# Choosing the experts of the last block's second and third tile beside the dense experts

## The chip, the cores and the metric

The kernel runs on one core of a Trainium2 chip. The metric is the device time of one execution in microseconds (us), lower is better.

## The reference

One decoder layer is computed for 1024 prompt tokens and 64 sample tokens, model width 1024, all in float32. A recurrent branch and a windowed attention branch are merged into a residual stream `hres`. Then comes the part that this change touches, an expert layer in which every token takes 8 heads times 16 experts out of 128 x 128, each expert being one row of `expert_u` and one of `expert_v`:

```python
s = einsum('nhpd,hpkd->nhpk', qr, sub_keys)           # two scores lists of 128 per head
s_top, i_top = top_k(s, 16)
cand = s_top[:, :, 0, :, None] + s_top[:, :, 1, None, :]
best, pos = top_k(cand, 16)                            # 16 of the pairs
idx = take_along_axis(i_top[0] * 128 + i_top[1], pos)  # 128 experts of a token
g = softmax(best)
act = gelu(einsum('cd,ced->ce', xt, expert_u[idx])) * g
y = hres + einsum('ce,ced->cd', act, expert_v[idx])
```

## The kernel before

**Blocks and tiles.** The tokens are worked through in three blocks (`BLOCKS`, line 42): 256 prompt tokens with the 64 sample tokens, then 384 and 384 prompt tokens. A tile is 128 tokens on the 128 partitions; the last block has three tiles. For each block the trunk (line 296) ends with `retrieve` (line 753), which leaves the two top-16 lists of each head and token in `v16` and `i16`.

**The choice.** `choose` (line 778) makes `idx` and `g` from these lists, one tile after the other. For a tile, DVE adds the pairs into `cd` and their indices into `ce` (line 799, 14 instructions), takes the best 16 for each of 8 heads with max, index and replace (lines 809 to 814, 64 instructions), and recovers the indices with a subtraction `eq` and a reduction `ev` for each head (lines 823, 825). A softmax follows (lines 834 to 839), with one exponential on ACT. For the last block the results go into the tiles `gA` and `iA` (lines 839, 841), which stay on the chip. `choose` is a generator with a `yield` after each head of either loop, 16 a tile. Its scratch tiles have one buffer each, so a tile's pieces wait for those of the tile ahead. In the first two blocks `behind` (line 992) lets it run next to the following block's trunk, there beside gathers for the sample tokens (`early_u`, line 962, and `early_v`, line 977).

**Two kinds of expert work.** The 640 prompt tokens of the first two blocks are done densely in `dense` (line 1014): all 128 groups of 128 experts are loaded, split into a high and a low part (`split`, line 160: high on ACT, low on POOL as `ul` and `vl`), and multiplied with all tokens on PE, three groups of experts in turn (`GRP`). DVE multiplies the scores with the routing weights (line 1052), makes the low part `al` (line 164), and adds the products into `dac` (lines 1070, 1072). The loads `un`, `vn` and `gt` are issued by SP.

The 384 tokens of the last block are done by gathering (`gather_steps`, line 876). For each tile there are 128 steps that fetch one row of `expert_u` for every token (an indirect DMA issued by POOL, line 888, four buffers `row`) and take its product with the token on DVE (line 890), and then 128 steps that fetch a row of `expert_v` (line 900) and add it into `acc` (line 902). A tile begins with a load of its tokens into `st` (line 881), which ACT copies to `xt` (line 883); it ends with ACT copying `acc` to `st` and SP storing it to `y` (line 906). `st` has two buffers.

**The order.** The code names `choose` for the whole last block first, in a pool of its own (`xp2`, line 1020), which is closed before the pool `gp` of the gathers is opened (line 1024), so that both lie in the same memory. Then comes the loop over the dense experts, and after each expert's `vl` a number of gather steps are named (`pump`, line 1062), 768 steps over 120 experts, with the rule that POOL takes them behind that `vl` (line 1061). The order on each engine's queue is set when the program is built: a scheduler plays a timeline and gives an engine, of the instructions that are ready, the one named first. On the chip each engine works through its own queue in that order.

Of the kernel before, what the change touches and what calls it, by code (L numbers as in the profile page):

```python
# [8 lines left out]
F32 = mybir.dt.float32  # L9
# [10 lines left out]
P = 128  # L20
D = 1024
# [11 lines left out]
NSLOT = PH * TOPK  # L33
# [8 lines left out]
BLOCKS = [(0, 256, True), (256, 640, False), (640, 1024, False)]  # L42
# [32 lines left out]
class Kern:  # L75
# [702 lines left out]
    def choose(self, bi):  # L778
# [6 lines left out]
        for t, (c0, r) in sorted(enumerate(tiles), key=lambda x: x[1][1]):  # L785
# [53 lines left out]
            nc.vector.tensor_tensor(gv[0:r], bv[0:r], sz[0:r].unsqueeze(2).to_broadcast([r, PH, TOPK]), op=ALU.mult)  # L839
            if r0 == RA:  # L840
                nc.vector.tensor_copy(self.iA[:, t], ev)
                continue
            e32 = xp.tile([P, NSLOT], I32, tag="bi", name="e32", bufs=1)
            nc.vector.tensor_copy(e32[0:r], ev[0:r].rearrange("p h s -> p (h s)"))
# [31 lines left out]
    def gather_steps(self, gp, gps):  # L876
        nc, i, o = self.nc, self.i, self.o
        for t in range(NA // P):

            st = gp.tile([P, D], F32, tag="st", name="st", bufs=2)  # L880
            nc.sync.dma_start(st, self.xn2n_d[t * P:(t + 1) * P, :])
            xt = gps.tile([P, D], F32, tag="gx", name="xt", bufs=1)
            nc.scalar.copy(xt, st)
            hv = gp.tile([P, NSLOT], F32, tag="hv", name="hv", bufs=2)
            ia = self.iA[:, t].rearrange("p h s -> p (h s)")
            for s in range(NSLOT):
                row = gp.tile([P, D], F32, tag="row", name="row", bufs=4)
                nc.gpsimd.indirect_dma_start(out=row, out_offset=None, in_=i["expert_u"],  # L888
                                             in_offset=bass.IndirectOffsetOnAxis(ap=ia[:, s:s + 1], axis=0))
                nc.vector.scalar_tensor_tensor(row, row, 1.0, xt, op0=ALU.mult, op1=ALU.mult, accum_out=hv[:, s:s + 1])  # L890
                yield
            nc.scalar.activation(hv, hv, AF.Gelu_apprx_tanh)
            nc.vector.tensor_tensor(hv, hv, self.gA[:, t].rearrange("p h s -> p (h s)"), op=ALU.mult)
            st = gp.tile([P, D], F32, tag="st", name="st", bufs=2)
            nc.sync.dma_start(st, self.hres_d[RA + t * P:RA + (t + 1) * P, :])
            acc = gps.tile([P, D], F32, tag="gx", name="acc", bufs=1)
            nc.scalar.copy(acc, st)
            for s in range(NSLOT):
                row = gp.tile([P, D], F32, tag="row", name="row", bufs=4)
                nc.gpsimd.indirect_dma_start(out=row, out_offset=None, in_=i["expert_v"],  # L900
                                             in_offset=bass.IndirectOffsetOnAxis(ap=ia[:, s:s + 1], axis=0))
                nc.vector.scalar_tensor_tensor(acc, row, hv[:, s:s + 1], acc, op0=ALU.mult, op1=ALU.add)  # L902
                yield
            st = gp.tile([P, D], F32, tag="st", name="st", bufs=2)
            nc.scalar.copy(st, acc)
            nc.sync.dma_start(o["y"][RA + t * P:RA + (t + 1) * P, :], st)

# [106 lines left out]
    def dense(self):  # L1014
        tc, nc, i, o = self.tc, self.nc, self.i, self.o
        halves = [(0, COL0[1]), (COL0[1], ND)]
        with ExitStack() as cx:
            up = cx.enter_context(tc.tile_pool(name="up", bufs=2))
            vp = cx.enter_context(tc.tile_pool(name="vp", bufs=GRP + 1))
            with tc.tile_pool(name="xp2", bufs=1) as self.xp:  # L1020
                for _ in self.choose(len(BLOCKS) - 1):
                    pass
            gps = cx.enter_context(tc.tile_pool(name="gps", bufs=1, space=PSUM))
            self.steps = self.gather_steps(cx.enter_context(tc.tile_pool(name="gp", bufs=1)), gps)
            ngat = 2 * NSLOT * (NA // P)
            done = 0
            psc = cx.enter_context(tc.tile_pool(name="dpsc", bufs=3, space=PSUM))
            pou = cx.enter_context(tc.tile_pool(name="dpou", bufs=3, space=PSUM))
            ac = [self.bp.tile([P, 4, ND], F32, tag="bl", name="dac0"), up.tile([P, 4, ND], F32, tag="dac", name="dac1", bufs=1)]
            groups = [list(range(s, min(s + GRP, P))) for s in range(0, P, GRP)]  # L1030
            for gi, grp in enumerate(groups):
                acts = []
                for e in grp:
                    uh = up.tile([P, KD, P], F32R, tag="uh", name="uh")
                    ul = up.tile([P, KD, P], F32R, tag="ul", name="ul")
                    un = up.tile([P, KD, P], F32, tag="raw", name="un", bufs=3)
                    nc.sync.dma_start(un, i["expert_uT"][e])
                    self.split(uh, ul, un, nc.gpsimd)
                    if e % 4 == 0:
                        gts = []  # L1040
                        for a, b in halves:
                            gts.append(up.tile([P, 12, 4, CH], F32, tag="gt", name="gt", bufs=3)[:, 0:(b - a) // CH])
                            nc.sync.dma_start(gts[-1], self.g_d[a // CH:b // CH, :, e:e + 4, :].rearrange("c j e n -> j c e n"))
                    ah = vp.tile([P, ND], F32R, tag="ah", name="ah")
                    al = vp.tile([P, ND], F32R, tag="al", name="al")
                    for (a, b), gt in zip(halves, gts):
                        ps = psc.tile([P, 512], F32, tag="sc", name="sc")
                        self.mm3(ps[:, 0:b - a], [(uh[:, k, :], ul[:, k, :], self.dx[k // 4][:, k % 4, a:b], self.dx[2 + k // 4][:, k % 4, a:b]) for k in range(KD)])
                        ge = ps[:, 0:b - a]
                        nc.scalar.activation(ge, ge, AF.Gelu_apprx_tanh)  # L1050
                        gv = ge.rearrange("j (c n) -> j c n", n=CH)
                        nc.vector.tensor_tensor(gv, gv, gt[:, :, e % 4, :], op=ALU.mult)
                        self.split(ah[:, a:b], al[:, a:b], ge)
                    vh = vp.tile([P, D], F32R, tag="vh", name="vh")
                    vl = vp.tile([P, D], F32R, tag="vl", name="vl")
                    vn = up.tile([P, D], F32, tag="raw", name="vn", bufs=3)
                    nc.sync.dma_start(vn, i["expert_v"][e * P:(e + 1) * P, :])
                    vsub = self.split(vh, vl, vn, nc.gpsimd)
                    acts.append((vh, vl, ah, al))
                    want = min(ngat, -(-ngat * (e + 1) // PACE))  # L1060
                    with tc.issue_after(vsub.ins):
                        self.pump(want - done)
                    done = max(done, want)
                for k in range(KD):
                    c = slice(k * P, (k + 1) * P)
                    for a, b in halves:
                        ps = pou.tile([P, 512], F32, tag="ou", name="ou")
                        self.mm3(ps[:, 0:b - a], [(vh[:, c], vl[:, c], ah[:, a:b], al[:, a:b]) for vh, vl, ah, al in acts])
                        if gi == 0:
                            nc.vector.tensor_copy(ac[k // 4][:, k % 4, a:b], ps[:, 0:b - a])  # L1070
                        else:
                            nc.vector.tensor_tensor(ac[k // 4][:, k % 4, a:b], ac[k // 4][:, k % 4, a:b], ps[:, 0:b - a], op=ALU.add)  # L1072
            for _ in self.steps:
                pass

            for t0 in range(0, ND, P):
                r = P
                y0 = t0 if t0 < COL0[1] else t0 - COL0[1] + ROW0[1]
                yt = up.tile([P, D], F32, tag="raw", name="yt", bufs=3)
                nc.sync.dma_start(yt[0:r], self.hres_d[y0:y0 + r, :])  # L1080
                for h in range(2):
                    pt = psc.tile([P, 4, P], F32, tag="sc", name="tr")
                    for k in range(4):
                        nc.tensor.transpose(pt[0:r, k, :], ac[h][:, k, t0:t0 + r], self.ident)
                    ys = yt[0:r, h * 512:(h + 1) * 512]
                    nc.vector.tensor_tensor(ys, ys, pt[0:r].rearrange("p k d -> p (k d)"), op=ALU.add)
                nc.sync.dma_start(o["y"][y0:y0 + r, :], yt[0:r])
# [116 lines left out]
```

## Time and profile before

| | us |
|---|---|
| median of 3 runs | 3814.39 |
| lowest of them | 3812.35 |
| the profiled execution, its own time | 3815.67 |
| its span, first to last instruction | 3813.9 |

| engine | busy over the span |
|---|---|
| PE (TensorE, products) | 3395.1 us, 89% |
| DVE (VectorE) | 2890.5 us, 76% |
| POOL (GpSimd) | 1535.9 us, 40% |
| ACT (ScalarE) | 1454.7 us, 38% |

The execution took 3815.67 us, 1.77 us more than its span. The trunk lasts to about 1820 us of the span; the dense experts and the gathers fill the rest. Times in rows are us from the span's start unless marked ns. In a row of a timeline stand start, duration, engine, line, operation, tile written and tiles read, and in brackets how long the engine had been idle and what ended that. In a row of stretches, the numbers behind those of the engines are the granted clock of PE, the mean busy share of the DMA engines and the GB/s they moved.

### The profile page before, as it was taken

To read this page: it belongs to the slowest core of one execution; us is meant where nothing else is said; L and a number is where in the kernel's file an instruction comes from. 1 tells how busy PE (TensorE), PEld (TensorE's weight loads), DVE (VectorE), ACT (ScalarE), POOL (GpSimd) and SP (SyncE) were. 2 spreads that over 40 slices of the span, in tenths; PEclk is the share of its full clock that TensorE was granted. 3 is DMA by queue.
4 is the path that set the end of the run, shared out by engine and by line. 5 is a ranking of instruction groups with operands and counts; after the bars stand their busy time and mean duration, and the time that the engine had idled before them with its cause. 6 is when DMAs were issued, how large, how long until landed. Compare 5 with 4: busy or idle time off the path is not lost.

```text
span 3813.9 us, 59344 instructions
## 1 busy us (share of the span) xinstructions
PE 3395.1 (89%) x21891; PEld 3238.4 (85%) x21891; DVE 2890.5 (76%) x6727; ACT 1454.7 (38%) x2969; POOL 1535.9 (40%) x1240
## 2 busy tenths in 40 slices
PE   6899989778898988678899999999999999999990
PEld 6789978668895878677799999999999999999990
DVE  6566897998789974557977776777777777777786
ACT  4565454446755372774322222222222222222210
POOL 0011100440000222000357776777767776777764
PEclk8899999889998999888899999999999999999995
DMA  6388823776561999654358988899888998998988
GB/s 227 121 258 283 263 77 106 251 233 199 187 210 44 305 311 343 212 189 143 123 203 312 324 304 290 305 318 324 304 299 305 314 322 316 315 323 311 309 293 282
DMA packets 539235, 968.36 MB, mean 254 GB/s; under 512 B 38108, under 2 KB 356508, under 8 KB 535840
## 3 DMA queue, kind: packets, MB, share of 16 engines
q0 software_dynamic: 141120, 513.86, 37.6%
q1 hardware_dynamic: 397824, 450.70, 36.9%
q8 instruction: 172, 2.82, 0.3%
q14 instruction: 119, 0.97, 0.1%
HBM read 860.10 MB, written 105.99 MB: 253 GB/s over the span
## 4 chain that ended last, share of the span: by engine, by line
PE 39%; DMA 20%; DVE 17%; issue 11%; POOL 7%; ACT 6%; SPq 0%; POOLq 0%; DVEq 0%; ACTq 0%
DMA row<-in_expert_v,iA 7%; PE mm L183 6%; PE mm L185 6%; PE mm L184 6%; DMA row<-in_expert_u,iA 4%; PE ou L183 3%; PE ou L184 3%; PE ou L185 3%; PE sc L183 2%; PE sc L184 2%; PE sc L185 2%; POOL row L888 2%; DVE acc L902 2%; PE tr L922 2%; ACT oij L942 2%
## 5 line engine op out<-in xcount | busy, mean ns | idle before, releaser
L183 PE MATMUL ou<-ah,vh 128*128 128x256 f32 (+1 forms) x2048 | 633.3, 314 | 47.2 <-ACT ah L163 27.8
L183 PE MATMUL sc<-dx,uh 128*128 128x256 f32 (+1 forms) x2048 | 636.1, 311 | 13.7 <-ACT uh L163 8.7
L184 PE MATMUL ou<-al,vh 128*128 128x256 f32 (+1 forms) x2048 | 632.5, 311 | 3.1 <-DVE al L164 2.9
L185 PE MATMUL sc<-dx,ul 128*128 128x256 f32 (+1 forms) x2048 | 634.3, 310 | 1.0 <-POOL ul L164 1.0
L184 PE MATMUL sc<-dx,uh 128*128 128x256 f32 (+1 forms) x2048 | 634.9, 310 | 0.0
L185 PE MATMUL ou<-ah,vl 128*128 128x256 f32 (+1 forms) x2048 | 630.7, 310 | 0.0
L902 DVE SCALAR_TENSOR_TENSOR acc<-row,hv,acc 128x1024 f32<-128x1024 f32 x384 | 493.9, 1286 | 146.7 <-DMA row<-in_expert_v,iA 138.4
L890 DVE SCALAR_TENSOR_TENSOR row<-row,xt 128x1024 f32<-128x1024 f32 x384 | 465.5, 1217 | 149.0 <-DMA row<-in_expert_u,iA 134.7
L900 POOL DMA_INDIRECT row<-in_expert_v,iA x384 | 360.7, 939 | 278.8 <-DVE acc L902 199.6
L164 POOL TENSOR_TENSOR ul<-un,uh 128x1024 fp32r<-128x1024 f32 x128 | 308.6, 2411 | 384.1 <-DMA gt<-g_d 303.6
L888 POOL DMA_INDIRECT row<-in_expert_u,iA x384 | 360.8, 940 | 247.7 <-DVE row L890 176.5
L183 PEld LDWEIGHTS ou<-ah,vh 128*128 128x128 f32 x2048 | 385.7, 190 | 63.1 <-ACT ah L163 33.8
L183 PEld LDWEIGHTS sc<-dx,uh 128*128 128x128 f32 x2048 | 391.6, 191 | 15.4 <-ACT uh L163 9.0
L184 PEld LDWEIGHTS ou<-al,vh 128*128 128x128 f32 x2048 | 389.7, 191 | 5.4 <-DVE al L164 4.8
L185 PEld LDWEIGHTS sc<-dx,ul 128*128 128x128 f32 x2048 | 390.8, 191 | 1.5 <-POOL ul L164 1.5
L184 PEld LDWEIGHTS sc<-dx,uh 128*128 128x128 f32 x2048 | 391.3, 191 | 0.0
L185 PEld LDWEIGHTS ou<-ah,vl 128*128 128x128 f32 x2048 | 389.0, 190 | 0.0
L1072 DVE TENSOR_TENSOR dac<-dac,ou 128x384 f32<-128x384 f32 (+1 forms) x672 | 315.4, 482 | 44.1 <-PE ou L185 39.5
L164 POOL TENSOR_TENSOR vl<-vn,vh 128x1024 fp32r<-128x1024 f32 x128 | 310.2, 2430 | 32.9 <-ACT vh L163 30.6
L163 ACT CAST uh<-un 128x1024 fp32r<-128x1024 f32 x128 | 134.4, 1050 | 453.3 <-PE sc L184 298.5
L977 POOL DMA_INDIRECT et<-in_expert_v,est x64 | 71.6, 1119 | 582.7 <-ACT ah L163 389.5
L183 PE MATMUL mm<-xh,whi 128*128 128x384 f32 (+1 forms) x768 | 259.5, 338 | 18.6 <-ACT Ti L687 15.3
(294 smaller groups left out, 7657.5 us busy)
## 6 DMA issues: line engine op xcount, KB each, us to landing
wraw<-in_w_in SPq DMA_DIRECT2D x132, 512.0 KB
un<-in_expert_uT SPq DMA_DIRECT2D x128, 512.0 KB
vn<-in_expert_v SPq DMA_DIRECT2D x128, 512.0 KB
lo_d<-wlo POOLq DMA_DIRECT2D x84, 512.0 KB
wlo<-lo_d SPq DMA_DIRECT2D x84, 512.0 KB
g_d<-sg SPq DMA_DIRECT2D x20, 2048.0 KB
wraw<-in_peer_w_query SPq DMA_DIRECT2D x48, 512.0 KB
gt<-g_d SPq DMA_DIRECT2D x32, 768.0 KB
```

The source lines that it names most:

```text
L163: nc.scalar.copy(hi, src)
L164: return (lo_eng or nc.vector).tensor_tensor(lo, src, f32(hi), op=ALU.subtract)
L183: nc.tensor.matmul(ps, lh, rh, start=first and j == 0, stop=False)
L184: nc.tensor.matmul(ps, lh, rl, start=False, stop=False)
L185: nc.tensor.matmul(ps, ll, rh, start=False, stop=last and j == n - 1)
L888: nc.gpsimd.indirect_dma_start(out=row, out_offset=None, in_=i["expert_u"], in_offset=bass.IndirectOffsetOnAxis(ap=ia[:, s:s + 1], axis=0))
L890: nc.vector.scalar_tensor_tensor(row, row, 1.0, xt, op0=ALU.mult, op1=ALU.mult, accum_out=hv[:, s:s + 1])
L900: nc.gpsimd.indirect_dma_start(out=row, out_offset=None, in_=i["expert_v"], in_offset=bass.IndirectOffsetOnAxis(ap=ia[:, s:s + 1], axis=0))
L902: nc.vector.scalar_tensor_tensor(acc, row, hv[:, s:s + 1], acc, op0=ALU.mult, op1=ALU.add)
L922: nc.tensor.matmul(pt[:, x, :], oj[:, x], wi[:, x], start=True, stop=True)
L942: nc.scalar.activation(wi[:, x], oi[:, :, x], AF.Copy, scale=sT[:, 2, n0 + x:n0 + x + 1])
L1072: nc.vector.tensor_tensor(ac[k // 4][:, k % 4, a:b], ac[k // 4][:, k % 4, a:b], ps[:, 0:b - a], op=ALU.add)
```

## The change

The choice of the last block's first tile stays ahead of the dense experts. Those of the second and third tile become steps that are named inside the loop, two after each dense expert, behind its gather steps. For that the generator gives out a word when a tile is finished, and the scratch pool `xp2` stays open to the end, so that the gathers' pool `gp` gets memory of its own. `st` and `hv` in `gather_steps` have one buffer in place of two.

```diff
             if r0 == RA:
                 nc.vector.tensor_copy(self.iA[:, t], ev)
+                yield "tile"
                 continue
...
-            st = gp.tile([P, D], F32, tag="st", name="st", bufs=2)
+            st = gp.tile([P, D], F32, tag="st", name="st", bufs=1)
             nc.sync.dma_start(st, self.xn2n_d[t * P:(t + 1) * P, :])
...
-            hv = gp.tile([P, NSLOT], F32, tag="hv", name="hv", bufs=2)
+            hv = gp.tile([P, NSLOT], F32, tag="hv", name="hv", bufs=1)
...
-            st = gp.tile([P, D], F32, tag="st", name="st", bufs=2)
+            st = gp.tile([P, D], F32, tag="st", name="st", bufs=1)
             nc.sync.dma_start(st, self.hres_d[RA + t * P:RA + (t + 1) * P, :])
...
-            st = gp.tile([P, D], F32, tag="st", name="st", bufs=2)
+            st = gp.tile([P, D], F32, tag="st", name="st", bufs=1)
             nc.scalar.copy(st, acc)
             nc.sync.dma_start(o["y"][RA + t * P:RA + (t + 1) * P, :], st)
...
-            with tc.tile_pool(name="xp2", bufs=1) as self.xp:
-                for _ in self.choose(len(BLOCKS) - 1):
-                    pass
+
+            self.xp = cx.enter_context(tc.tile_pool(name="xp2", bufs=1))
+            choice = self.choose(len(BLOCKS) - 1)
+            for x in choice:
+                if x == "tile":
+                    break
             gps = cx.enter_context(tc.tile_pool(name="gps", bufs=1, space=PSUM))
...
                     done = max(done, want)
+                    for _ in range(2):
+                        next(choice, None)
```

## Rows read from the trace of the kernel before

**Rows 1.** windows: busy us (count) of PE, PEld, DVE, ACT, POOL.

```profile
1819.00:1944.00 125.00, 110.34 (x699) 107.11 (x700) 123.18 (x374) 40.86 (x60) 46.20 (x18) 0.92 0.36 112
1850.00:1950.00 100.00, 94.88 (x629) 92.31 (x630) 95.38 (x266) 31.68 (x50) 36.22 (x17) 1.00 0.28 92
2000.00:3700.00 1700.00, 1659.90 (x11153) 1644.81 (x11151) 1291.68 (x2152) 419.13 (x703) 1208.11 (x928) 0.99 0.90 311
```

**Rows 2.** the chain of waits, 3725 to 3810, its shares by line.

```profile
by line: DMA row<-in_expert_v,iA 61.4%; issue 19.1%; DVE acc L902 15.3%; POOL row L900 4.9%; ACT st L905 1.2%; POOLq L900 0.2%; DVEq L902 0.2%
```

**Rows 3.** the timeline of POOL: start us, us, instruction, idle before it.

```profile
1944.37 0.94 POOL L888 DMA_INDIRECT row<-in_expert_u,iA  x1 [0.35 <-DVE iA L841]
...
3725.91 0.94 POOL L900 DMA_INDIRECT row<-in_expert_v,iA  x1 [2.51 <-DVE acc L902]
...
3802.75 0.94 POOL L900 DMA_INDIRECT row<-in_expert_v,iA  x1 [1.31 <-DVE acc L902]
```

**Rows 4.** gathers alone (tile row), DVE and POOL busy us (count) by stretch.

```profile
2000.00:3700.00 1700.00, 870.18 (x1062) 654.93 (x697) 0.99 0.90 311
3725.00:3810.00 85.00, 56.06 (x44) 37.46 (x40) 0.52 0.85 295
```

**Rows 5.** timeline of DVE during the choice: start us, us, instruction.

```profile
1832.66 2.83 DVE L799 TENSOR_TENSOR cd<-v 128x128 f32<-128x128 f32 x4
...
1835.61 2.54 DVE L799 TENSOR_TENSOR cd<-v 128x24 f32<-128x24 f32 x3
...
1852.65 1.40 DVE L834 COPY sz<-bv 128x8 f32<-128x8 f32 x1
...
1873.87 0.21 DVE L841 CAST iA<-ev 128x128 int32<-128x128 f32 x1
```

**Rows 6.** the dense experts' groups on DVE, 1816 to 1946: busy us, mean ns.

```profile
L1052 DVE TENSOR_TENSOR sc<-sc,gt 128x256 f32<-128x256 f32 (+1 forms) x17 | 8.2, 482 | 0.0
L164 DVE TENSOR_TENSOR al<-sc,ah 128x256 fp32r<-128x256 f32 (+1 forms) x16 | 7.6, 475 | 0.5 <-ACT ah L163 0.5
L1070 DVE COPY dac<-ou 128x256 f32<-128x256 f32 (+1 forms) x16 | 7.5, 476 | 0.0
L1072 DVE TENSOR_TENSOR dac<-dac,ou 128x256 f32<-128x256 f32 (+1 forms) x16 | 7.5, 475 | 0.0
```

**Rows 7.** line 823 in two stretches (640 to 900, 1816 to 1946), durations min/median/max.

```profile
L823 DVE TENSOR_TENSOR eq<-ce,bf x19: 971/986/997, 640.1 to 898.7; 128x800 f32<-128x800 f32 x11, 64x800 f32<-64x800 f32 x8
L823 DVE TENSOR_TENSOR eq<-ce,bf x24: 973/989/2989, 1838.7 to 1938.8; 128x800 f32<-128x800 f32 x24
```

**Rows 8.** page groups: gather issues beside a choice (L977), without one (L888).

```profile
L888 POOL DMA_INDIRECT row<-in_expert_u,iA x384 | 360.8, 940 | 247.7 <-DVE row L890 176.5
...
L977 POOL DMA_INDIRECT et<-in_expert_v,est x64 | 71.6, 1119 | 582.7 <-ACT ah L163 389.5
```

**Rows 9.** the timelines of SP and ACT where tile buffer st is used.

```profile
1944.12 0.33 SPq L881 DMA_DIRECT2D st<-xn2n_d  x1
...
1947.70 1.02 ACT L883 COPY xt<-st 128x1024 f32<-128x1024 f32 x1 [2.34 <-DMA st<-xn2n_d]
...
2579.98 0.70 SPq L881 DMA_DIRECT2D st<-xn2n_d  x1
...
2584.29 5.64 SPq L906 DMA_DIRECT2D out_y<-st  x1
...
2588.38 1.02 ACT L883 COPY xt<-st 128x1024 f32<-128x1024 f32 x1 [3.84 <-DMA st<-xn2n_d]
...
3810.32 0.33 SPq L906 DMA_DIRECT2D out_y<-st  x1
```

**Rows 10.** the timelines of PE and SP at the end of the dense experts.

```profile
3721.22 0.34 PE L185 MATMUL ou<-ah,vl 128*128 128x384 f32 x1
...
3739.26 2.90 SPq L1087 DMA_DIRECT2D out_y<-yt  x2
```

**Rows 11.** waits of PE, 1944 to 3722: us in total, times, longest.

```profile
PE ou L183 <- ACT ah L163: 24.2, 19, 4.5
```

## The prediction

> **What bounds the kernel now.** I read the end first, since only what ends last can shorten the time. The chain of waits over the last 85 us is made of the gathers: 61.4% of it is a row of `expert_v` in flight, 15.3% the addition on it [rows 2]. PE's last product of the dense experts starts at 3721.2 [rows 10], while the last gather is issued at 3802.8 [rows 3]. So PE is done some 80 us before the end, and what is left is a tail of gathers.
>
> Next I ask what paces the gathers. Between 2000 and 3700 POOL issues 697 of them in 1700 us, one per 2.44 us; in the tail 40 in 85 us [rows 4], or, from the issue at 3725.91 to the last at 3802.75, 39 intervals in 76.84 us, 1.97 us each [rows 3]. No engine on their path is full in the long stretch: DVE is busy 1291.68 of 1700 us (76%), POOL 1208 (71%), the DMA engines 0.90 [rows 1]. A gather goes round a loop of four buffers (issue, flight, DVE, issue again), and that loop runs at a steady rate from its first turn. Its end is then its start plus 768 turns plus what interrupts it.
>
> So the start counts. The first gather is issued at 1944.37 and had waited for `iA` of line 841 [rows 3], which is the third tile's. The first tile's `iA` was there at 1873.87 [rows 5]. In between the DMA engines stand idle for the most part: 0.36 from 1819 to 1944 [rows 1].
>
> **The change, part by part.**
>
> *The gathers start earlier.* They need the first tile's choice alone. In the trace that tile shares DVE with the second tile's choice: the latter's pair sums (2.83 and 2.54 us) and a copy (1.40) stand ahead of 1873.87 [rows 5], 6.8 us that now come later. That puts `iA` at 1867 and the first gather at 1867.5, 77 us earlier. Least: 70.5, if nothing gets out of its way. Most: DVE is busy 123.2 us from 1819 to 1944 [rows 1], the dense experts' part of it is 8.2 + 7.6 + 7.5 + 7.5 = 30.8 [rows 6], so the choice costs 92.4 us, 31 a tile; with 5 us of dense work in between it would end at 1855, 89 us earlier. I take 77, for it removes only what I can point at.
>
> *The choice of two tiles moves.* That is 62 us of DVE, some 100 instructions a tile, and one exponential a tile on ACT, which is idle three quarters of the time [rows 1]; it issues no DMA and nothing on SP, POOL or PE. DVE idles 24% of the long stretch, so 62 us need 258 us of it, until about 2125, in which 106 gathers fall. The second tile's rows are wanted only after 256 gathers, so nobody waits for the result. What it costs is delay: a row that has landed finds a choice instruction running in 24% of cases and waits half of its 0.985 us [rows 7], 0.12 us, over 106 gathers 12 us. Least 0, if the loop's slack absorbs it; most 62, if DVE's time is taken from the gathers one for one. I take 12, as the idle share is there in the row.
>
> *Gather issues beside a choice.* In the trunk, where a choice runs beside gathers, an issue takes 1119 ns on the mean, against 940 beside the dense experts alone [rows 8]. 0.18 us over 106 gathers is 19 us if each is felt; with four in flight a quarter, 5. Range 0 to 19.
>
> *One buffer `st`.* Between two tiles the store of `y` and the load of the next tokens now follow each other in one buffer. Before, the load was issued at 2579.98, ahead of the store at 2584.29, and ACT could copy it at 2588.38 [rows 9]. Now the load waits on SP until the store has landed. A store in a quiet moment takes 3.6 us (issued at 3810.32, span's end 3813.9), a load 3.6 (1944.12 to 1947.70), the load in the crowd 8.4 (2579.98 to 2588.38) [rows 9]. So the copy comes at 2591.5 to 2601.1 in place of 2588.4: 3 to 13 us, at two boundaries 6 to 25. I take 20, near the crowded end, since the DMA engines are at 0.90 there. Loads `un` and `vn` queue behind this wait on SP. That can delay PE, whose cover is its 80 us of lead. The load of `hres` inside a tile is free to go once `xt` is copied, 128 gathers ahead: nothing. `hv` in one buffer: written and read by DVE in order: nothing.
>
> *PE.* Gathers now run from 1867, in a stretch in which PE was busy 94.9 of 100 us beside a DVE at 95%, against 97.6% later [rows 1]. In the long stretch its largest wait is 24.2 us in all, on ACT's `ah` [rows 11]. I leave its end where it is; ten us more would still lie under the tail.
>
> *The sum.* -77 + 12 + 5 + 20 = -40 us in the gathers' loop, at 2.44 us a turn 16.4 gathers more by PE's end. They are missing in the tail, at 1.97 us: 32 us. From the profiled 3815.67 that gives 3783; its time lies 1.3 us above the median of 3814.39, so **3782**. The ends: -89 + 0 + 0 + 6 = -83, 34 gathers, 67 us, 3747; and -70.5 + 62 + 19 + 25 = +35.5, 14.5 gathers, 29 us slower, 3843.
>
> **A rule against the change.** `eq` reads two tiles of SBUF. Beside gather issues alone it took at most 997 ns; beside POOL's splits up to 2989 [rows 7]. So the gathers don't hold it up, and the splits, as frequent before as after, do; that is in the 92.4 us. The Trainium skill (SBUF — State Buffer, "Who interferes with whom") says that a DVE instruction with two SBUF inputs contends with a GpSimd instruction that reads SBUF, and that the second to start is blocked until the first is through. If that held for the gathers' issues too, each of the some 50 two-input instructions of two tiles could lose up to 0.94 us, which would add 47 us to the sum's -40 and leave no gain. The trace agrees for the splits and, by the 997 ns, not for the issues.
>
> **The rivals.**
>
> *The tail vanishes (12%).* DVE's idle time takes the choice without touching a gather, and `st` costs little: the favourable ends above, 3747. There a floor is met, too: the last dense rows of `y` are stored from 3739.26 over 2.90 us [rows 10], and 3.6 us for landing give 3746 in the span. For it: 24% idle. Against: 1119 ns instead of 940. Faster than 3738, 2% below, it can be only if PE also ends earlier, for which the trace has few waits to give back.
>
> *DVE becomes the bound beside the choice (13%), slower.* Place: the first 260 us after 1867. The two steps after each expert are named ahead of the next expert's gather steps; if the queue puts them in front of rows that have landed, the gathers lose all 62 us there, 19 at their issue and 25 at the boundaries: -77 + 106 = +29 us, 12 gathers, 23 us: 3837. It decides from the point where that stretch loses more than 77 - 25 = 52 us, 21 of its 106 gathers. For it: from 1819 to 1944 the choice, named first, held DVE at 98.5% [rows 1]. Against: now the earlier gathers are named ahead of it. Should the gathers' issues also hold up the choice's two-input instructions (25 a tile, up to 0.94 us each), 47 us more of DVE are at stake: with all else as forecast -40 + 47 = +7 us, 3820. I give that 3 of the 13%, as the 997 ns speak against it [rows 7].
>
> *The gathers don't start earlier (5%).* Something else holds them to 1944, such as the new place of their buffers or the queue order on POOL. Then only `st` remains: 20 us, 8 gathers, 16 us: 3830. The DVE release in [rows 3] speaks against it.
>
> **How the numbers follow.** My forecast has 65%: 3782, in its own range 3755 to 3808. The rivals have 12, 13 and 5%, and 5% is left to a reordering of the queues that I can't see, on either side. The range of 8 in 10 is 3746 to 3818: the forecast with the vanished tail, up to a little above the time before, leaving out most of the slower cases and what lies under the floor. 2% is 76 us, about what a measurement of this kernel can tell from no change; faster than 3738 gets 0.07, slower than 3891 gets 0.05, within gets 0.88.
>
> **What would show it.** The first gather at 1860 to 1870; one gather per 2.5 to 2.6 us until about 2125, then 2.44; the first copy to `xt` of the next tile 10 us after the store's issue; PE's last product near 3722; a tail of about 35 gathers behind it. Wrong would be: a first gather at 1944, fewer than 85 gathers in the 260 us from 1867, or PE ending later than 3760.

## The result: 1.0% faster, near the forecast

Over 13 runs each the changed kernel takes 3773.45 us in the median, the kernel before 3808.72: 35 us less, or 39 us by the ratio of 0.9898, 95% interval 0.9879 to 0.9917. One run of each is a slow one (10178.95 and 7936.55 us) and stays out of the ratio; the others lie between 3756 and 3781 and between 3789 and 3823. The gain is under 2%. The forecast was 3782 in a range of 3746 to 3818. The profiled executions took 3777.02 us (span 3775.2) and 3815.67 (span 3813.9), 38.7 us apart; the comparisons of rows below are made on these two.

### The profile after

Stretches of the changed kernel, columns as in [rows 1]; the second is the one with gathers and choice side by side:

```profile
1819.00:1944.00 125.00, 106.70 (x660) 102.92 (x660) 118.57 (x369) 37.13 (x56) 72.33 (x47) 0.91 0.74 243
1868.00:2042.00 174.00, 151.37 (x953) 146.38 (x953) 170.06 (x364) 40.25 (x65) 111.93 (x84) 0.93 0.82 270
2000.00:3700.00 1700.00, 1658.78 (x11144) 1642.59 (x11142) 1302.42 (x2128) 422.13 (x707) 1209.28 (x925) 0.99 0.90 310
```

Until 1944 the DMA engines, idle in [rows 1] at 0.36, are now at 0.74. The timeline of POOL shows why: the first gather, and the last.

```profile
1868.64 0.94 POOL L889 DMA_INDIRECT row<-in_expert_u,iA  x1 [10.30 <-DVE iA L841]
...
3762.97 0.94 POOL L901 DMA_INDIRECT row<-in_expert_v,iA  x1 [0.39 <-DVE acc L903]
```

Against [rows 3] the first starts 75.7 us earlier and the last 39.8. The gathers alone, as in [rows 4]:

```profile
1867.00:2125.00 258.00, 116.88 (x193) 98.51 (x99) 0.95 0.84 280
2000.00:3700.00 1700.00, 864.59 (x1027) 651.90 (x693) 0.99 0.90 310
```

One per 2.45 us in the long stretch, as before (2.44). By 3700 us 741 gathers have been issued, before it was 717. The chain from 3700 to 3775, by line:

```profile
by line: issue 38.3%; DMA row<-in_expert_v,iA 34.1%; POOL row L901 12.3%; DVE acc L903 7.7%; ACT st L906 1.3%; DVE dac L1078 1.3%; POOL vl L164 0.6%; POOLq L901 0.3%; POOLq L164 0.1%; DVEq L903 0.1%
```

It still ends in rows of `expert_v`, but their flight is 34.1% of it in place of 61.4% [rows 2]: the dense experts now reach far into this stretch. The last addition to `dac`, on the timeline of DVE, before and after, and the last stores of `y` after, on SP's:

```profile
3722.68 0.56 DVE L1072 TENSOR_TENSOR dac<-dac,ou 128x384 f32<-128x384 f32 x1
```

```profile
3741.48 0.55 DVE L1078 TENSOR_TENSOR dac<-dac,ou 128x384 f32<-128x384 f32 x1
```

```profile
3757.61 2.93 SPq L1093 DMA_DIRECT2D out_y<-yt  x2
...
3771.62 0.33 SPq L907 DMA_DIRECT2D out_y<-st  x1
```

So PE's end comes 19 us later. Where it lost time, by the waits of PE from 1868 to 2042 (us in total, times, longest):

```profile
PE ou L183 <- DVE dac L1078: 16.2, 10, 6.5
PE ou L183 <- DVE dac L1076: 3.7, 3, 2.2
```

PE waits for `dac` additions, which stand on DVE's queue among choice instructions. What the choice displaced on DVE is seen in its largest group in the first 174 us of gathers, before (1945 to 2119) and after (1868 to 2042); the last field is the idle time ahead of it and what ended that:

```profile
L890 DVE SCALAR_TENSOR_TENSOR row<-row,xt 128x1024 f32<-128x1024 f32 x67 | 81.2, 1217 | 30.5 <-DMA row<-in_expert_u,iA 28.7 <-issue 1.6
```

```profile
L891 DVE SCALAR_TENSOR_TENSOR row<-row,xt 128x1024 f32<-128x1024 f32 x62 | 74.5, 1209 | 3.5 <-DMA row<-in_expert_u,iA 3.5
```

Before, DVE stood 28.7 us in front of rows in flight; after, 3.5. The choice took that time, and five rows fewer were worked off. The gathers still end last, but not by much: the last dense rows are stored by 3760.5, the last gathered tile 11 us later, at 3771.62. Before, it was 68 us later, at 3810.32 for 3742.2 [rows 9, rows 10].

### The profile page after: what moved, and what is told of

The parts are those of the page before. It is cut to its first block, busy times and chain, and to the rows that moved or that the text cites. A ratio compares the mean times of both kernels' runs of the same rounds, so it can differ in the third digit from the quotient of the medians.

```text
span 3775.2 us, 59354 instructions
## 1 busy us (share of the span) xinstructions
PE 3401.7 (90%) x21891; PEld 3244.8 (86%) x21891; DVE 2889.4 (77%) x6727; ACT 1453.8 (39%) x2969; POOL 1539.4 (41%) x1240
## 5 line engine op out<-in xcount | busy, mean ns | idle before, releaser
L978 POOL DMA_INDIRECT et<-in_expert_v,est x64 | 71.6, 1119 | 585.0 <-DVE oi L940 389.6
```

Source lines behind the costliest of these rows:

```text
L978: nc.gpsimd.indirect_dma_start(out=row(s), out_offset=None, in_=self.i["expert_v"], in_offset=bass.IndirectOffsetOnAxis(ap=self.es[:, 0, s ...
```

## The experiments

The theory is the prediction's: a loop of four row buffers goes round in 2.44 us, and the end is its start, 768 turns and what interrupts it. The rival that the trace after suggests (the prediction's loop is called theory B where both are named, this one A): the end follows PE, which the choice delays. In the changed kernel and its relatives the end lies some 30 us behind the last addition to `dac`, and on POOL's queue, whose order is written when the program is built, 18 gathers stand behind the last `vl` in place of 51.

**e2_onebuf**: the kernel before with one buffer.

```diff
-            st = gp.tile([P, D], F32, tag="st", name="st", bufs=2)
+            st = gp.tile([P, D], F32, tag="st", name="st", bufs=1)
```

> The kernel before with st and hv in one buffer and nothing else of the change: the whole choice still stands ahead. My theory: the two boundaries take some 12 us each in place of 6.3 and 4.5, 14 us more in the gathers' loop, 5 to 6 gathers more in the tail, 11 us slower: 3820 against 3809, ratio 1.003. Rival (the boundary costs nothing): ratio 1.000, and stops that are longer but made good by a shorter wait of the rows behind them.

Measured 1.0029 (1.0014 to 1.0044), 11 us more, as expected for this run; the prediction's 20 us of the loop make 8 gathers or 16 us. In its profiled execution the stops at the two boundaries, from the last addition to the next tile's first product, grow to 15.9 and 13.0 us, but 718 gathers are issued by 3700, before it was 717. So the loss shows in the times alone.

**e1_rowstore**: the changed kernel, the last copy of a tile through a row buffer, so that `st` is free for the next load.

```diff
-            st = gp.tile([P, D], F32, tag="st", name="st", bufs=1)
-            nc.scalar.copy(st, acc)
+            yo = gp.tile([P, D], F32, tag="row", name="yo", bufs=4)
+            nc.scalar.copy(yo, acc)
```

> The changed kernel, but the store of y at a tile's end goes through one of the four row buffers, so that st is free and the next tile's tokens can be loaded ahead of the boundary again. My theory (the gathers' loop sets the end, and each of the two boundaries with one st stops it for some 12.4 us from the last sum to the first product, against 6.3 and 4.5 us with two): the stops fall to 4 to 7 us, some 14 us of loop come back, about 5 gathers, 10 us of the end: 3763 where the changed kernel takes 3773, ratio to before 0.988. PE's last product stays near 3740. Rival (the rows already in flight cover the boundary, or the kernel's end is by now set by PE and the stores of the dense rows behind it, at some 3764): the stops shrink and the time stays at 3773.

Measured 0.9893 (0.9877 to 0.9910). The copy to `xt` now comes 1.1 and 2.3 us behind the copy out, in place of 11.2 and 11.3, and the stops shrink from 12.3 and 12.4 us to 2.7 and 6.4, yet 739 gathers are issued by 3700, not more than 741. That is the rival's case; the time alone, with 0.988 inside the interval, would not tell. `yo` occupies one of the four row buffers while its store is in flight; whether that takes the gain back was not tried.

**e3_nochoice**: the changed kernel without the choice of the second and third tile; they use the first tile's experts, so that part of the computation is left out.

```diff
-            ia = self.iA[:, t].rearrange("p h s -> p (h s)")
+            ia = self.iA[:, 0].rearrange("p h s -> p (h s)")
...
-                    for _ in range(2):
-                        next(choice, None)
```

> The changed kernel without the choice of the second and third tile: their rows are fetched with the first tile's choice, so that everything but these 62 us of DVE and two exponentials stays. It measures what the choice costs beside the dense experts. My theory (DVE is full for 174 us after the first gather; the price falls on PE, which loses some 16 us there waiting for dac, and on the gathers, which lose some 5 to 7 turns): PE ends at 3720 to 3725 in place of 3740, 72 gathers in the first 174 us in place of 66, the end 12 to 17 us earlier: 3758, ratio 0.987. Rival (the choice is free in DVE's idle time): PE ends at 3740 again and the time is 3773. Second rival (the choice is what holds the gain back): 3740 or less.

Measured 0.9812 (0.9799 to 0.9826), 33 us below the changed kernel by the ratios; the profiled span is 3733.1, 42 us below. That is the second rival's number. The stretch from 1868 to 2042:

```profile
1868.00:2042.00 174.00, 172.45 (x1169) 171.09 (x1168) 133.45 (x260) 41.26 (x70) 126.25 (x97) 1.00 0.91 319
```

PE is busy 172.45 us in place of 151.37, and in the first 300 us from the first gather 128 are issued in place of 118. By 3700 it is 760 in place of 741. The choice costs far more than the 12 to 17 us forecast for it. PE's share in this is not waiting alone: it makes 1169 products here and 953 in the changed kernel, and 216 products of 0.148 us (172.45 over 1169) are 32 us, of which it stood idle for 21. The other 11 fit the granted clock, 0.93 in place of 1.00: 7% of 174 us are 12. That all tiles fetch the same experts here is not what makes it faster: inside a tile and past the choice a turn takes 2.42 us (2500 to 3100), in the changed kernel 2.41 (2545 to 3140).

**e5_behind_al**: one step of the choice per expert, on DVE's queue behind that expert's `al`.

```diff
-                        self.split(ah[:, a:b], al[:, a:b], ge)
+                        asub = self.split(ah[:, a:b], al[:, a:b], ge)
...
-                    for _ in range(2):
+                    with tc.issue_after(asub.ins):
                         next(choice, None)
```

> The changed kernel with the choice spread out: one step per expert, and each step put on DVE's queue behind the low part al of that expert, so that the choice takes 34 experts instead of ending 174 us after the first gather. Same work, half the density. My theory: DVE is no longer full (some 85 to 90% until about 2350), PE loses 3 to 6 us there in place of 16, PE ends at 3728 to 3732, the gathers lose about as many turns or a few less: 3765 to 3772, ratio 0.989. Rival (PE's lost time has another cause, the gathers beside the first experts): PE ends at 3740 as before, 3773. Second rival (the order of DVE's queue is now worse for the rows): slower than 3780.

Measured 0.9874 (0.9856 to 0.9892). The choice now ends at 2319.9 in place of 2041.5; PE is busy 168.49 of the 174 us, its last addition to `dac` is back at 3722.71, and 747 gathers are issued by 3700. Spread out, the choice costs PE less. In the time the gain on the changed kernel is not clear: the two intervals overlap.

**e4_twoahead**: two tiles named ahead of the dense experts, the third beside them.

```diff
+            left = 2
             for x in choice:
-                if x == "tile":
+                left -= x == "tile"
+                if left == 0:
                     break
```

> The changed kernel, but two tiles are chosen ahead of the dense experts and only the third beside them. Theory A (PE and POOL's queue): in all kernels so far the end lies 55 to 60 us behind the last expert's `vl` on POOL where 18 to 21 gathers are queued behind it, and 116 us where there are 51; so it follows PE, which the choice beside it delays by DVE. Half of the choice gives back half of PE's 19 us: the last addition to `dac` near 3732, the last `vl` near 3709, again 18 gathers queued behind it, end 3764 in the span, ratio 0.987, although the first gather is 38 us later, near 1906. Theory B (the prediction's: a loop of four buffers that counts from the first gather): 38 us later at the start, 8 us back from the half choice, 30 us at 2.44 a turn are 12 gathers, 24 us: 3799, ratio 0.997.

Measured 0.9869 (0.9848 to 0.9891), but the edit did not do what it says. The three `iA` are written at 1875.1, 1965.4 and 2046.3, in the changed kernel at 1868.2, 1964.6 and 2041.5, and the first gather follows at 1875.56, not near 1906. By these times DVE has nearly the same order whichever tile is named where. So the second tile named ahead does not hold the gathers back, and it is hardly the naming inside the loop that starts them early, but what else is in the change: `gp` no longer lies in the memory of the scratch pool. SP's load of `st`, which reads nothing of the choice, points the same way. Before, it was issued at 1944.12 [rows 9], right behind the third tile's `iA`; in the changed kernel, on SP's timeline:

```profile
1824.63 0.43 SPq L882 DMA_DIRECT2D st<-xn2n_d  x1
```

All three tiles named ahead with separate memory was not run. The run tells nothing about half a choice, and that theory A's 0.987 was met is no support for it.

**e9_half**: e5_behind_al with a step for every second expert.

```diff
-                        next(choice, None)
+                        for _ in range(e % 2):
+                            next(choice, None)
```

> The changed kernel with one step of the choice for every second expert, on DVE's queue behind that expert's `al`: half the pace of e5_behind_al. Theory A: the choice takes PE's time where it stands in front of additions to `dac`; spread over some 68 experts it is 6% of DVE beside 77%, and PE's loss of 22 us (e5_behind_al against e3_nochoice) falls to about half: last addition to `dac` near 3711, 21 gathers behind the last `vl`, span 3747, ratio 0.984. Theory B: the first gather and the sum of the choice are those of e5_behind_al, so the time is too: ratio 0.987 to 0.988.

Measured 0.9873 (0.9853 to 0.9894): the same as e5_behind_al. Its last addition to `dac` came at 3727.64, not 3711. Theory B's number held, and A's 0.984 lies outside the interval. PE ends 14 us earlier here than in the changed kernel, yet the last gather, at 3762.41, comes when it did there (3762.97); the profiled execution is the longest of its four, though.

**e12_forced_before** and **e13_forced_e5**: POOL's queue fixed so that no gather stands behind the last `vl`, in the kernel before and in e5_behind_al.

```diff
+                self.lastg = nc.gpsimd.indirect_dma_start(out=row, out_offset=None, in_=i["expert_v"],
...
-                    vsub = self.split(vh, vl, vn, nc.gpsimd)
+                    with tc.issue_after(self.lastg.ins) if e > 8 else ExitStack():
+                        vsub = self.split(vh, vl, vn, nc.gpsimd)
...
-                    want = min(ngat, -(-ngat * (e + 1) // PACE))
+                    want = min(ngat, -(-ngat * max(0, e - 7) // 119))
```

> The kernel before, its choice left as it was, but with POOL's queue fixed so that every expert's `vl` stands behind the gathers named with the expert ahead of it: no gather stands behind the last `vl` in place of 51. The gathers named per expert are 768 over 119 experts from the ninth on. Theory A: 51 is a matter of the order written, not of what the loop can do; PE goes on at its pace, the last `vl` stays near 3698, and the end comes 44 us later with the last dense rows of `y`: span 3743, ratio 0.982. Theory B: the loop does a turn in 2.44 us and no faster beside the dense experts; 768 turns from 1944 end at 3818, PE is held up through `vl`, and the end comes 44 us behind that: span 3862, ratio 1.012.

> e5_behind_al (the choice one step per expert behind its `al`) with the same order on POOL: every `vl` behind the gathers named with the expert ahead of it, 768 over 123 experts from the fifth on, none behind the last `vl` in place of 21. Theory A: last `vl` near 3699 as in e5_behind_al, end 44 us later: span 3743, ratio 0.984. Theory B: 768 turns of 2.44 us from 1864 end at 3738, PE is held up to that, end 44 us later: span 3782, ratio 0.993.

Measured 1.0014 (0.9997 to 1.0032) and 1.0013 (0.9994 to 1.0033). Theory A's 0.982 and 0.984 fell; B's 1.012 and 0.993 were off, too. The last gather of e12_forced_before, on POOL, and PE's largest wait from 2350 to 3700 (in the kernel before it is 7.3 us for `dac` and 14.6 for `ah`):

```profile
3765.21 0.94 POOL L900 DMA_INDIRECT row<-in_expert_v,iA  x1 [0.59 <-DVE acc L902]
```

```profile
PE ou L183 <- DVE dac L1073: 41.4, 52, 2.8
```

From 1944.57 that is 2.37 us a turn, in the kernel before 2.42 from first to last. The forced order speeds the loop by 2%, and PE pays for it: its last `vl` comes at 3768.34, not near 3698, its last addition to `dac` at 3786.68, 64 us later than before, and the execution ends with the dense rows 15 us behind that. In e13_forced_e5 a `vl` that waited 14.1 us for ACT's `vh` also held the first gather back, to 1895.67, and the last addition came at 3818.24. The order on POOL makes no room: what the gathers gain by it PE loses, and the time stays.

**e10_pe_before** and **e11_pe_after**: 19 us more of PE, late in the dense experts, in both kernels.

```diff
-                        self.mm3(ps[:, 0:b - a], [...])
+                        for _ in range(2 if e in (60, 75, 90) else 1):
+                            self.mm3(ps[:, 0:b - a], [...])
```

> The kernel before, with the score products of experts 60, 75 and 90 made twice (the second writes the same result): 3 x 6.4 = 19 us more of PE, nothing more on DVE, the DMA queues or POOL. POOL's queue, written anew for it, has 36 gathers behind the last `vl` in place of 51. Theory B (the gathers' loop counts): gathers go on while PE works longer, the end stays: ratio 1.000, 720 gathers by 3700. Theory A (gathers in step with PE): the last `vl` comes at 3697.5 + 19 = 3716.5, and 36 gathers behind it at 1.97 us: 11 us earlier, ratio 0.997. If PE's time lies on the path whatever the queue: 19 us later, 1.005.

> The changed kernel with the same 19 us more of PE; its queue on POOL has 6 gathers behind the last `vl` in place of 18. Theory B: the end is that of the gathers, 741 by 3700 and 27 left, and stays within 4 us: ratio 0.990 to 0.991. Theory A: the end follows PE, whose last addition to `dac` moves from 3741 to 3760; the dense rows of `y` end 20 us behind that, 3782 to 3794 with the rest: ratio 0.992 to 0.995.

Measured 1.0019 (0.9999 to 1.0039) and 0.9897 (0.9862 to 0.9931), the latter the changed kernel's own ratio.

In e10_pe_before PE's end moves by 23 us, to 3745.50, and 720 gathers are issued by 3700, as theory B said; theory A's 0.997 and the 1.005 of PE on the path lie outside the interval. In the kernel before, the end does not follow PE.

e11_pe_after does not decide it for the changed kernel. The last addition to `dac` and the last gather, on the timelines of DVE and POOL, of e11_pe_after, and its last stores of `y` on SP's:

```profile
3762.54 0.55 DVE L1079 TENSOR_TENSOR dac<-dac,ou 128x384 f32<-128x384 f32 x1
```

```profile
3752.83 0.94 POOL L901 DMA_INDIRECT row<-in_expert_v,iA  x1 [1.18 <-DVE acc L903]
```

```profile
3763.11 0.34 SPq L907 DMA_DIRECT2D out_y<-st  x1
...
3773.15 1.64 SPq L1094 DMA_DIRECT2D out_y<-yt  x2
```

PE's end moves by 21 us, the span only from 3775.2 to 3778.1. But the last gather comes 10 us earlier than in the changed kernel, with 6 of them behind the last `vl` as expected, and the last stores are now those of the dense rows (`yt`): PE has used up the room that the gathers' end left it, and ends the execution itself. The interval holds part of theory A's 0.992 to 0.995, too. What speaks against theory A for the changed kernel is that the last gather does not go with PE's end. With PE's last addition at 3722.71, 3727.64, 3741.48 and 3762.54 it comes at 3746.12, 3762.41, 3762.97 and 3752.83 (e5_behind_al, e9_half, the changed kernel, e11_pe_after). That the end lies some 30 us behind PE's end in several kernels may come from both sharing POOL's and DVE's queues; no run shows that.

**e8_both**: e5_behind_al with e1_rowstore.

> e5_behind_al and e1_rowstore together: the choice one step per expert behind `al`, and the final copy of a tile through a row buffer. If the stops between tiles cost what the loop loses in them, some 11 us of 14 come back, 4 to 5 gathers, 9 us: ratio 0.985. If the gathers move in step with PE through POOL's queue, as e1_rowstore suggests, nothing comes back: 0.987.

Measured 0.9885 (0.9855 to 0.9916), 740 gathers by 3700: no gain beyond e5_behind_al's that shows. Here, too, PE's last addition comes early, at 3729.64, and the last gather at 3762.36.

**e7_fiverows**: the changed kernel with five row buffers in one set, which also serve the loads and final copies that used `st`.

```diff
-            st = gp.tile([P, D], F32, tag="st", name="st", bufs=1)
+            st = gp.tile([P, D], F32, tag="row", name="st", bufs=5)
...
-                row = gp.tile([P, D], F32, tag="row", name="row", bufs=4)
+                row = gp.tile([P, D], F32, tag="row", name="row", bufs=5)
```

> The changed kernel with one set of five row buffers for the gathered rows, the tokens' loads and the final copies, in place of four rows and one `st`. If four buffers in flight are what sets 2.44 to 2.47 us a gather (the prediction's loop), a fifth lets a turn fall to 2.44 x 4 / 5 = 1.95 at best; the gathers then have no part in the end, 3700 sees all 768 of them issued, PE's last addition to `dac` stays near 3741 and the end is 20 us later with the dense rows of `y`: 3763 or less, ratio 0.986. If DVE and the DMA engines set the pace, which gathers and dense experts share, the turn stays at 2.4 to 2.5 us, 735 to 745 gathers are issued by 3700, and the time is that of the changed kernel or, as no gather is queued behind the last `vl` and PE is held up in its place, up to that of before: ratio 0.990 to 1.000.

Measured 3699.04 us, 0.9706 (0.9675 to 0.9737): 113 us faster than before, and below every other version. The stretch from 2400 to 3400 in the changed kernel, and here:

```profile
2400.00:3400.00 1000.00, 973.35 (x6547) 964.03 (x6547) 754.34 (x1274) 250.45 (x417) 710.50 (x543) 0.99 0.90 311
```

```profile
2400.00:3400.00 1000.00, 996.46 (x6787) 994.64 (x6786) 799.46 (x1358) 257.48 (x429) 752.19 (x582) 1.00 0.94 332
```

The same stretch, DVE's groups on gathered rows, in the changed kernel and here:

```profile
L891 DVE SCALAR_TENSOR_TENSOR row<-row,xt 128x1024 f32<-128x1024 f32 x229 | 277.3, 1218 | 96.7 <-DMA row<-in_expert_u,iA 89.9 <-ACT xt L884 6.3
L903 DVE SCALAR_TENSOR_TENSOR acc<-row,hv,acc 128x1024 f32<-128x1024 f32 x178 | 228.8, 1285 | 70.4 <-DMA row<-in_expert_v,iA 69.4
```

```profile
L891 DVE SCALAR_TENSOR_TENSOR row<-row,xt 128x1024 f32<-128x1024 f32 x256 | 309.0, 1214 | 58.4 <-DMA row<-in_expert_u,iA 58.0
L903 DVE SCALAR_TENSOR_TENSOR acc<-row,hv,acc 128x1024 f32<-128x1024 f32 x183 | 234.9, 1284 | 49.7 <-DMA row<-in_expert_v,iA 48.8
```

And its last gather and last addition to `dac`:

```profile
3600.87 0.94 POOL L901 DMA_INDIRECT row<-in_expert_v,iA  x1 [0.30 <-issue]
```

```profile
3682.03 0.55 DVE L1078 TENSOR_TENSOR dac<-dac,ou 128x384 f32<-128x384 f32 x1 [0.30 <-PE ou L185]
```

From the first gather at 1864.19 a turn takes 2.26 us, in the changed kernel 2.47: the four buffers did set the pace, though a fifth gives 8%, not the 20% of the upper bound. Most of this is not at the boundaries: inside a tile a turn takes 2.25 us (3040 to 3590) in place of 2.41 (3170 to 3690). All gathers are issued 81 us before PE ends, so here PE ends last. It gains as well, which neither theory had: DVE stands 107 us in front of rows in flight in this stretch in place of 159, and in that time the additions and `al` behind such a row wait, too. That this is why PE gains was not tried by itself, but it fits its waits: those for `ah` and `dac` ahead of its products `ou`, 18.2 and 7.7 us from 2350 to 3550 in the changed kernel, shrink to 1.4 and 2.1. The loads through row buffers came in the same edit; e1_rowstore shows that the final copies alone give nothing, the loads alone were not tried, but inside a tile they play no part.

## Why the prediction was right, and where it was not

**What bounds the kernel: right.** e7_fiverows and e10_pe_before show both halves of it: a wider loop ends sooner, and more work for PE alone moves nothing in the kernel before. The traces give a plain rule: the execution ends with the later of two ends, 11 to 12 us behind the last gather (in the kernel before, the changed one and eight others) or 15 to 16 behind PE's last addition to `dac` (in e7, e11, e12 and e13). After the change the gathers are last only just: by this rule PE's cover has shrunk from some 75 us to 18, between the last stores from 68 to 11.

**The earlier start: right in size.** 1868.64 for 1867.5. Behind it lay a gain that the prediction did not see. Before, POOL's queue had three splits ahead of the fifth gather, one of them waiting 7.15 us for ACT's `uh`:

```profile
1948.11 0.94 POOL L888 DMA_INDIRECT row<-in_expert_u,iA  x1 [0.31 <-issue]
1949.06 2.40 POOL L164 TENSOR_TENSOR ul<-un,uh 128x1024 fp32r<-128x1024 f32 x1
1951.42 2.40 POOL L164 TENSOR_TENSOR vl<-vn,vh 128x1024 fp32r<-128x1024 f32 x1
1960.97 2.40 POOL L164 TENSOR_TENSOR ul<-un,uh 128x1024 fp32r<-128x1024 f32 x1 [7.15 <-ACT uh L163]
1963.51 0.94 POOL L888 DMA_INDIRECT row<-in_expert_u,iA  x1
```

In the first 20 us 5 gathers were issued, in the changed kernel 10: 5 x 2.44 = 12 us.

**The choice in DVE's idle time: the term that was mis-sized.** The prediction charged 12 us for delay and 5 for slower issues, 17 over the choice's stretch, "as the idle share is there in the row". Read against the loop before, the count agrees: 99 gathers from 1867 to 2125 in place of 106, 7 x 2.44 = 17 us. But that loop carried the 12 us of its own late start. Against e3_nochoice, which starts as briskly (10 gathers in the first 20 us), the first 300 us hold 10 gathers fewer, 24 us, and the first gather itself comes 9 us later. What the term missed: the idle 24% was in good part DVE standing in its own queue in front of a row in flight (28.7 of some 50 idle us in the first 174), not room at the disposal of others. A choice instruction there delays the row that lands meanwhile and the `dac` additions behind it.

**Issues beside the choice.** The group of the page that answers to [rows 8]:

```profile
L889 POOL DMA_INDIRECT row<-in_expert_u,iA x384 | 366.4, 954 | 279.5 <-DVE row L891 193.2
```

954 ns on the mean against 940, 5.4 us over all 384: the 1119 ns of the trunk did not carry over. The rule weighed in the prediction: `eq` beside the choice's stretch, as in [rows 7].

```profile
L823 DVE TENSOR_TENSOR eq<-ce,bf x16: 974/988/3861, 1885.0 to 2033.7; 128x800 f32<-128x800 f32 x16
```

Five of the 16 run into a split on POOL and take 2.08 to 3.86 us; the other eleven, ten of them beside a gather's issue, 0.97 to 1.04. The issue is what gives way there: on POOL's timeline,

```profile
1885.17 1.65 POOL L889 DMA_INDIRECT row<-in_expert_u,iA  x1 [0.52 <-DVE bv L835]
```

falls into an `eq` from 1885.02 to 1886.01 and takes 1.65 us in place of 0.94. The Trainium skill (SBUF — State Buffer, "Who interferes with whom") says that the instruction that starts second is blocked until the first is through. The trace agrees for five of the seven issues that start inside one of these eleven `eq` (1.22 to 1.65 us; the other two, at its very start and end, take 0.94), and for three of the five splits, which run when the `eq` starts. It does not agree for the other two, where the split starts 0.16 and 0.58 us behind the `eq`, and still it is the `eq` that gives way. These rows of DVE and POOL show the first:

```profile
1920.92 3.43 DVE L823 TENSOR_TENSOR eq<-ce,bf 128x800 f32<-128x800 f32 x1
```

```profile
1921.08 2.41 POOL L164 TENSOR_TENSOR ul<-un,uh 128x1024 fp32r<-128x1024 f32 x1
```

Nor does it agree for an `eq` that starts during an issue, as at 1948.32: it is not blocked and takes its 0.98 us.

**One buffer `st`: near.** SP's and ACT's timelines at the first boundary:

```profile
2521.08 0.34 SPq L907 DMA_DIRECT2D out_y<-st  x1
2528.10 0.33 SPq L882 DMA_DIRECT2D st<-xn2n_d  x1
```

```profile
2531.27 1.02 ACT L884 COPY xt<-st 128x1024 f32<-128x1024 f32 x1 [3.75 <-DMA st<-xn2n_d]
```

The copy comes 10.2 us after the store's issue, 10 were forecast. From the last addition to `acc` to the next tile's first product it is 12.3 and 12.4 us, before 6.2 and 4.4: 14 us more at both, for 20. How much of this reaches the end is open: e2_onebuf shows 11 us in the time, e1_rowstore takes 16 us of the stops away and gains no gather.

**PE: the step that failed, at no cost.** "I leave its end where it is; ten us more would still lie under the tail." It ended 19 us later, by its waits for `dac` and a lower granted clock. The tail behind its last product, at 3740.01, is 9 gathers, where some 35 behind 3722 were forecast. The 19 us still lay under the tail, with 11 to 18 to spare; the 21 us more of e11_pe_after did not. Nor did the remark hold that PE has few waits to give back: with five buffers its last addition came at 3682.03, 41 us before that of the kernel before, and the time fell below the floor of 3746.

**The sum.** Measured terms: -75.7 - 12 + 24 + 14 = -50 us, 20 gathers at 2.44; 24 more were issued by 3700, for 16.4 forecast. Four of them, 10 us, stay unexplained, or more if part of the 14 does not count. At the 2.02 us of the tail before (51 gathers from 3700 to the last at 3802.75) 24 are 48 us. The 27 left take 2.33 us each, as the dense experts run on beside them, 8 us more: 40, for 38.7 measured and 32 forecast. That 32 came this near is in part luck: the 12 us at the start that nobody saw made up for the 7 by which the choice was too cheap, and runs of one kernel lie up to 34 us apart. Of the rivals, the one with DVE as the bound named the right place, and its price was between the forecast's and its own; the gain at the start outweighed it.

## What to carry to other kernels

An engine's idle share is not free room when the idle time lies in front of data in flight: its queue is in order, and what is put there delays what lands next and all that stands behind it. Look at what ended the idle time before work is moved into it. And where a loop of a few buffers sets the pace, another buffer can be worth more than an earlier start: here a fifth gave some 74 us on top of the 39 of the change, it seems partly because the engine that waits less for data serves the others sooner.

## What the runs showed that was not expected

- 19 us more of PE work cost nothing that shows in the kernel before (1.0019), though PE is busy 1660 of 1700 us [rows 1]. In the changed kernel they cost nothing either (0.9897), but used up what PE had to spare.
- A fixed distance between two ends is no proof that one drives the other: the rule that the end lies 55 us behind the last `vl` where 18 gathers are queued fitted e4_twoahead (54.6), and the forecast that theory A made with it for e12_forced_before, 3743, was 58 us off (3801.5). What failed there was not the distance, 33 us behind the last `vl` for the 44 forecast, but where that `vl` came: theory A left it in its place, and it came some 70 us later.
- In the stretch from 1868 to 2042 the granted clock, a mean over its two levels of 1.2 and 2.4 GHz, is 0.93 in the changed kernel, where PE waited up to 6.5 us at a time for DVE, and 1.00 in e3_nochoice, where it was busy 172.45 of 174 us.
